# A transformer block on one core: the wide group of the down projection in reverse order, separate buffers for weight sums, a fifth place for split weights, and VectorE in place of GpSimd behind the direct down tiles

## The chip, the core and the metric

The kernel runs on one core of a Trainium2 chip. TensorE (PE in the profile) multiplies, with its weight loads shown as PEld; VectorE (DVE), ScalarE (ACT) and GpSimd (POOL) work elementwise; SyncE (SP) issues nearly all transfers. Each engine runs its own instructions strictly in order, and they wait for each other by semaphores. Tiles lie in SBUF (128 partitions); products accumulate in eight PSUM banks. The metric is the device time of one execution in microseconds. Three runs of the kernel before took 1105.82, 1107.14 and 1108.59 us.

## The reference

One encoder layer on 256 tokens and 16 meta tokens, 2048 channels, all in float32:

```
h = concat(meta, x)
hn = rmsnorm(h);  proj = hn @ w_in
out_a = neighbourhood attention, out_b = latent attention
h = h + concat(rmsnorm(out_a), rmsnorm(out_b)) @ w_out
x2 = rmsnorm(h)
gc = conv_b + sum_i conv_w[i] * shifted(x2 @ w_gate)     # width 3
h = h + (silu(gc) * (x2 @ w_up)) @ w_down                # 5632 inner columns
return h without the meta rows
```

The change touches the last part, above all `@ w_down`: 5632 = 44 x 128 rows of weights, 2048 = 16 x 128 output columns.

## The kernel before

**Split weights.** Each float32 weight is taken apart into a high part of reduced width (`whi`, written by ScalarE, L250) and a low part (`wlo`, the weight minus its high part, written by VectorE, L254). A product of a weight block and an activation is then three products: high x high, high x low, low x high. Weights come in pieces of up to 1024 columns. A piece is loaded into a weight buffer (`raws`; tiles named `raw`, `more_raw`, `halves`), then split by `split_hi` and `split_lo` into one of four places of each kind (`his`, `los`); the weight buffer is free when the low part is done, the place when TensorE has used it. Late in the kernel there are fourteen weight buffers: five `raw`, one `more_raw`, and eight in `halves`, memory that the activations of the gate and up products leave.

**Seven products for eight.** A part of `w_up` and of `w_down` is computed by a scheme with seven block products in place of eight, which needs sums of weight quarters (`weight_sums`, VectorE additions) and sums of activations (`value_sums`, stored in DRAM as `s_up` and `s_down` and loaded again into the tiles `sin` and `sums`, the slots `s_parts`). In `w_up` five groups of four output tiles are done in this way. `w_down` has three parts. The middle group (columns 1024 to 1535) and the wide group (columns 0 to 1023) use the scheme, in 22 row pairs each; the last four output tiles are done directly, m = 0 to 3, 44 blocks each ("direct tiles"). A wide pair has 512-column quarters and seven times three products (`MM`, L290). Its sums are partly made long before, in DRAM, and loaded (tiles `early`): an even pair ("both") loads two sums and computes one buffer of further ones, an odd pair ("third") loads one half and computes two buffers.

**Order.** TensorE's order is a list of pieces: gate and up tiles with the five groups mixed in, then gate and up mixed with the middle group, then the wide group mixed with the pieces of the direct tiles. All other engines' order comes from a planner (`Flow`): every piece of work is a thread that asks for buffers (`Slots`, first come first served), waits for events and then for an engine at an estimated cost; the planner always issues what can start first, by priority among equals. In `load_pair` a pair takes its buffers for weights and for sums together, when its first load is planned. The low-part split (`split_lo`) goes ahead of the sums when it is less than two or three pieces ahead of TensorE. `LANDING` is the planner's time for a load to arrive.

**Direct tiles.** Tiles 0 to 2 take two products a block (`mm2`, L2040 and L2041): the high weights against high and low activations side by side, 512 columns, then the low weights against 256. Tile 3 takes three products of 256 (`mm3`, L713 to L715). `down_out` ends a tile: for tiles 0 to 2 ScalarE copies both halves of the bank into row buffers (`mt`, twelve), GpSimd (L278) adds them, multiplies by the norm's scale and adds the residual; for tile 3 VectorE reads the bank, multiplies and adds. Then the row goes to DRAM.

Of the kernel before, what the change touches and what calls it, by code (L numbers as in the profile page):

```python
# [15 lines left out]
P = 128  # L16
# [201 lines left out]
def encoder_block(ctx: ExitStack, tc: tile.TileContext, io):  # L218
# [103 lines left out]


    combined = Slots(tiles(wpool, 1, [P, PW], "sums"))

# [50 lines left out]
    class RowPair:  # L376
# [55 lines left out]
    s_parts = Slots([])  # L432
    pieces = []
# [71 lines left out]
    def down_pairs(of, src, q):  # L505
        out = []
        for g in range(FC // 2):
            r = RowPair(src[g], g, q, of)
            r.first, r.last, r.near = g == 0, g == LAST, False
            out += [(p, "scheme", r, 0) for p in r.pieces]  # L510
        return out
# [47 lines left out]
    def load_pair(r):  # L559
        def load_S():  # L560
            if r.near:
                r.ev_S = ev_near[r.g]
                return
            if r.of == "mid" and r.g in last_S:
                yield last_S[r.g][1]
                r.S = last_S[r.g][0][0]
                fl.set(r.ev_S)
                return
            r.S = yield from one(s_parts)
            src, saved = saved_sums["up" if r.of == "up" else "down"][r.g]  # L570
            yield saved
            yield "sp", 600
            load(r.S, src, r.ev_S, nc.sync)

        q = r.q
        if r.wide:
# [36 lines left out]
    def weight_sums(r):  # L613
        yield r.loaded
        q = r.q
        if r.wide:
            low, up, t, m = (r.at[k] for k in ("lower", "upper", "two", "more"))
            if r.mode == "both":
                yield r.summed[0]
                yield from TT(m[:, :q], low[:, :q], t[:, :q], ALU.add)  # L620
# [3 lines left out]
            else:  # L624
                yield r.first_loaded
                yield from TT(m[:, :q], up[:, :q], up[:, q:], ALU.add)
# [6 lines left out]
            return  # L633
        t, raw = r.at["sums"], r.at["raw"]
        if r.mode == "third":
# [1236 lines left out]
    near, ev_near = [None] * (KC // 2), [Event() for _ in range(KC // 2)]  # L1872
    act = mts = None

    def mlp_buffers():

        nonlocal act, mts
        yield ev_s2t
# [75 lines left out]
    def value_sums(dst, saved, a, b, place=None):  # L1954
# [53 lines left out]
    def down_out(m, ps):  # L2008
        o = yield from one(mts)
        o_ = o[:, :SEQ]  # L2010
        if m < KC - ST - 1:
            t = yield from one(mts)
            yield from ACT(o_, ps[:, :SEQ], AF.Copy)
            yield from ACT(t[:, :SEQ], ps[:, SEQ:], AF.Copy)
            fl.put(acc, ps)
            yield from PTT(o_, t[:, :SEQ], o_, ALU.add)
            fl.put(mts, t)
            yield from PTT(o_, o_, s_2[:, :SEQ], ALU.mult)
            yield from PTT(o_, o_, hT[ST + m][:, :SEQ], ALU.add)
        else:  # L2020
            yield from TT(o_, ps[:, :SEQ], s_2[:, :SEQ], ALU.mult)
            fl.put(acc, ps)
            yield from TT(o_, o_, hT[ST + m][:, :SEQ], ALU.add)
        if m < KC - ST - 1:
# [22 lines left out]
    def mlp_weights():  # L2047
        pss, f = [], 0
        for p, kind, which, q in work:
# [57 lines left out]
    def scheme_products(p, r):  # L2107
# [31 lines left out]
        if p is r.pieces[-1]:  # L2139
            if not r.near:  # L2140
                if r.S is not near[-1]:
                    fl.put(s_parts, r.S)
# [301 lines left out]
```

## Time and profile before

| | |
|---|---|
| median of three runs | 1107.14 us |
| time of the profiled execution | 1107.99 us |
| its span | 1106.0 us |
| TensorE, VectorE, ScalarE, GpSimd busy | 99%, 92%, 68%, 14% |
| granted TensorE clock | 1.0 |
| moved by DMA | 265.35 MB, mean 240 GB/s |
| share of TensorE in the chain that ended last | 83% |

Busy shares are means over stages with different limits, so the stages have to be read one by one. The attention part lies before some 400 us, gate, up and the five groups up to 770, the middle group up to 942, the wide group with direct tiles from there to 1092, and the end of the last direct tile after it. A matmul's end is modelled and reaches over the start of the next, so that products which follow each other without a gap show a TensorE busy all the time; what a product costs is the distance between two starts.

### The profile page before, as it was taken

To read this page: it belongs to the slowest core of one execution; us is meant where nothing else is said; L and a number is where in the kernel's file an instruction comes from. 1 tells how busy PE (TensorE), PEld (TensorE's weight loads), DVE (VectorE), ACT (ScalarE), POOL (GpSimd) and SP (SyncE) were. 2 spreads that over 40 slices of the span, in tenths; PEclk is the share of its full clock that TensorE was granted. 3 is DMA by queue.
4 is the path that set the end of the run, shared out by engine and by line. 5 is a ranking of instruction groups with operands and counts; after the bars stand their busy time and mean duration, and the time that the engine had idled before them with its cause. 6 is when DMAs were issued, how large, how long until landed. Compare 5 with 4: busy or idle time off the path is not lost.

```text
span 1106.0 us, 22349 instructions
## 1 busy us (share of the span) xinstructions
PE 1095.7 (99%) x8164; PEld 1046.2 (95%) x8164; DVE 1016.9 (92%) x1922; ACT 750.8 (68%) x1514; POOL 149.6 (14%) x217
## 2 busy tenths in 40 slices
PE   9999999999999999999999999999999999999998
PEld 9999999999999999999999999999999999887777
DVE  8979888888878989999999999999999998999997
ACT  8788979798647776656656666665666665766664
POOL 3211222322433400000000000000000000304011
PEclk9999999999999999999999999999999999999999
DMA  8765678667877887665747668667888879699891
GB/s 325 253 230 175 194 226 228 173 195 183 257 204 209 237 283 270 213 205 184 255 161 227 208 208 276 216 220 258 277 307 295 286 260 359 233 337 318 274 313 62
DMA packets 82470, 265.35 MB, mean 240 GB/s; under 512 B 9304, under 2 KB 13016, under 8 KB 82360
## 3 DMA queue, kind: packets, MB, share of 16 engines
q1 hardware_dynamic: 78600, 254.08, 67.6%
q0 software_dynamic: 3472, 9.57, 5.4%
q8 instruction: 64, 1.05, 0.4%
q14 instruction: 46, 0.38, 0.1%
q10 hardware_dynamic: 288, 0.27, 0.1%
HBM read 245.39 MB, written 35.13 MB: 254 GB/s over the span
## 4 chain that ended last, share of the span: by engine, by line
PE 83%; DVE 7%; ACT 4%; DMA 3%; issue 2%; POOL 0%; DVEq 0%; SPq 0%; ACTq 0%; POOLq 0%
PE bank L290 23%; PE bank L713 15%; PE bank L714 15%; PE bank L715 15%; PE bank L2040 10%; PE bank L2041 5%; DVE wlo L254 4%; PE bank L296 2%; ACT whi L250 1%; DMA raw<-early 1%; DVE scr L262 1%; ACT scr L250 1%; DMA raw<-in_w_cq 1%; DMA halves<-early 1%; DVE halves L254 1%
## 5 line engine op out<-in xcount | busy, mean ns | idle before, releaser
L250 ACT ACTIVATE whi<-raw 128x512 fp32r<-128x512 f32 (+2 forms) x513 | 383.0, 767 | 152.4 <-PE bank L714 48.7
L254 DVE TENSOR_TENSOR wlo<-raw,whi 128x512 fp32r<-128x512 f32 (+2 forms) x513 | 445.1, 886 | 29.1 <-ACT whi L250 25.4
L713 PE MATMUL bank<-hl,whi 128*128 128x258 f32 (+1 forms) x1208 | 347.7, 288 | 0.0
L714 PE MATMUL bank<-hl,whi 128*128 128x258 f32 (+1 forms) x1208 | 343.7, 285 | 0.0
L715 PE MATMUL bank<-hl,wlo 128*128 128x258 f32 (+1 forms) x1208 | 343.3, 284 | 0.2
L715 PEld LDWEIGHTS bank<-hl,wlo 128*128 128x128 f32 x1208 | 229.7, 190 | 1.0 <-DVE wlo L254 0.6
L714 PEld LDWEIGHTS bank<-hl,whi 128*128 128x128 f32 x1208 | 229.3, 190 | 0.1
L713 PEld LDWEIGHTS bank<-hl,whi 128*128 128x128 f32 x1208 | 228.3, 189 | 0.4
L290 PE MATMUL bank<-whi,act 128*128 128x256 f32 (+1 forms) x600 | 152.9, 306 | 0.0
L2040 PE MATMUL bank<-hl,whi 128*128 128x512 f32 x384 | 136.5, 395 | 0.0
L290 PEld LDWEIGHTS bank<-whi,act 128*128 128x128 f32 x600 | 105.0, 189 | 6.2
L2041 PE MATMUL bank<-hl,wlo 128*128 128x256 f32 x384 | 107.6, 280 | 0.0
L278 POOL TENSOR_TENSOR mt<-mt,mt 128x256 f32<-128x256 f32 x3 | 13.5, 4496 | 646.6 <-ACT mt L250 646.6
L290 PE MATMUL bank<-wlo,act 128*128 128x256 f32 (+1 forms) x300 | 91.7, 306 | 0.0
L2040 PEld LDWEIGHTS bank<-hl,whi 128*128 128x128 f32 x384 | 72.1, 188 | 14.8
L250 ACT ACTIVATE whi<-halves 128x1024 fp32r<-128x1024 f32 (+1 forms) x68 | 62.4, 933 | 34.1 <-PE bank L290 16.7
L290 PE MATMUL bank<-whi,sin 128*128 128x256 f32 (+1 forms) x264 | 76.3, 333 | 0.0
L254 DVE TENSOR_TENSOR wlo<-halves,whi 128x1024 fp32r<-128x1024 f32 (+1 forms) x68 | 72.9, 1099 | 2.9 <-ACT whi L250 2.8
L2041 PEld LDWEIGHTS bank<-hl,wlo 128*128 128x128 f32 x384 | 72.4, 189 | 0.0
L250 ACT ACTIVATE whi<-more_raw 128x1024 fp32r<-128x1024 f32 (+2 forms) x58 | 49.9, 871 | 25.1 <-PE bank L714 9.3
L290 PEld LDWEIGHTS bank<-wlo,act 128*128 128x128 f32 x300 | 56.7, 189 | 2.8
L254 DVE TENSOR_TENSOR wlo<-more_raw,whi 128x1024 fp32r<-128x1024 f32 (+2 forms) x58 | 57.0, 994 | 2.4 <-ACT whi L250 2.4
(311 smaller groups left out, 2163.1 us busy)
## 6 DMA issues: line engine op xcount, KB each, us to landing
raw<-in_w_gate SPq DMA_DIRECT2D x74, 512.0 KB, 4.8
raw<-in_w_in SPq DMA_DIRECT2D x52, 512.0 KB, 4.9
raw<-in_w_up SPq DMA_DIRECT2D x43, 512.0 KB, 4.9
raw<-in_w_up_s SPq DMA_DIRECT2D x34, 512.0 KB, 4.4
raw<-in_w_out SPq DMA_DIRECT2D x32, 512.0 KB, 5.3
sin<-s_down SPq DMA_DIRECT2D x30, 512.0 KB, 6.5
s_down<-sums SPq DMA_DIRECT2D x22, 512.0 KB, 4.4
raw<-in_w_down_m SPq DMA_DIRECT2D x18, 512.0 KB, 5.5
```

What stands on the lines that cost most here:

```text
L250: nc.scalar.activation(out, in_, f, **kw)
L254: nc.vector.tensor_tensor(out, a, b, op)
L262: nc.vector.scalar_tensor_tensor(out, a, s, b, op0, op1)
L278: nc.gpsimd.tensor_tensor(out, a, b, op)
L290: nc.tensor.matmul(o, l, r, start=start, stop=stop)
L296: nc.tensor.transpose(o, i, ident[:n, :n])
L713: nc.tensor.matmul(ps, whi, xhi, start=start, stop=False)
L714: nc.tensor.matmul(ps, whi, xlo, start=False, stop=False)
L715: nc.tensor.matmul(ps, wlo, xhi, start=False, stop=stop)
L2040: nc.tensor.matmul(ps, whi, x, start=start, stop=False)
L2041: nc.tensor.matmul(ps[:, :n], wlo, x[:, 0, :], start=False, stop=stop)
```

## The change

- The wide group goes through its row pairs from the last (21) to the first (0). The activation sums of the pairs 19, 20 and 21, which the middle group has used last, stay in their three places (`kept_S`); they are no longer loaded for the wide group, and those of 20 and 21 are no longer saved.
- Weight sums get slots of their own, `made`: first `more_raw` alone, then also the last two of the eight in `halves`. `raws` keeps five, later eleven. A pair takes sum buffers when its sums are computed, not when it is loaded.
- Once the middle group's result is read from the banks, a thread takes all twelve row buffers, waits for the low part of the wide group's sixth piece, gives four back and turns the memory of the other eight into a fifth place for high parts and a fifth for low parts.
- Direct tiles 0 to 2 take three products a block and are ended by VectorE as tile 3 is.
- `LANDING` is 3200 instead of 2600.

```diff
-LANDING, SAVING = 2600.0, 2500.0
+LANDING, SAVING = 3200.0, 2500.0
+RING_AT = 5
...
+    made = Slots([])
...
-                fl.put(raws, self.at[kind])
+                by_sums = kind in ("more", "sums") or kind == "two" and self.mode == "third"
+                fl.put(made if by_sums else raws, self.at[kind])
...
-        for g in range(FC // 2):
+        order = range(FC // 2) if of == "mid" else range(LAST, -1, -1)
+        for g in order:
...
+                kept_S[r.g] = r
+                fl.set(ev_kept[r.g])
+                return
+            if r.of == "down" and r.g > LAST - 3:
+                yield ev_kept[r.g]
+                r.ev_S = kept_S[r.g].ev_S
+                r.S = kept_S[r.g].S
                 return
...
-            r.at["two"], r.at["more"] = yield raws, 2
             if r.mode == "both":
+                r.at["two"] = yield from one(raws)
...
-            r.at["raw"], r.at["sums"] = yield raws, 2
+            r.at["raw"] = yield from one(raws)
...
+            if r.mode == "both":
+                yield r.summed[0]
+                r.at["more"] = yield from one(made)
+            else:
+                yield r.first_loaded
+                r.at["two"], r.at["more"] = yield made, 2
...
-            fl.put(raws, t[:, a : a + PW])
+            fl.put(raws if 2 * i + a // PW < 8 - 2 else made, t[:, a : a + PW])
...
-        mts = Slots(tiles(mpool, 12, [P, NT], "mt"))
+        mt_rows[:] = tiles(mpool, 3, [P, 4 * NT], "mt")
+        mts = Slots([t[:, i * NT : (i + 1) * NT] for t in mt_rows for i in range(4)])
...
-            fl.put(raws, t)
+            fl.put(made, t)
...
-        fl.spawn(save_sums(dst, saved, parts, place is None and not last))
+        if not last:
+            fl.spawn(save_sums(dst, saved, parts, place is None))
...
-        if m < KC - ST - 1:
-            t = yield from one(mts)
-            yield from ACT(o_, ps[:, :SEQ], AF.Copy)
-            yield from ACT(t[:, :SEQ], ps[:, SEQ:], AF.Copy)
-            fl.put(acc, ps)
-            yield from PTT(o_, t[:, :SEQ], o_, ALU.add)
-            fl.put(mts, t)
-            yield from PTT(o_, o_, s_2[:, :SEQ], ALU.mult)
-            yield from PTT(o_, o_, hT[ST + m][:, :SEQ], ALU.add)
-        else:
...
+        yield from TT(o_, ps[:, :SEQ], s_2[:, :SEQ], ALU.mult)
+        fl.put(acc, ps)
+        yield from TT(o_, o_, hT[ST + m][:, :SEQ], ALU.add)
...
-                    if which < KC - ST - 1:
-                        yield from mm2(ps, act[:, f], SEQ, f == 0, f == FC - 1)
-                    else:
-                        yield from mm3(
-                            ps[:, :SEQ], act[:, f, 0, :], act[:, f, 1, :], f == 0, f == FC - 1
-                        )
+                    yield from mm3(
+                        ps[:, :SEQ], act[:, f, 0, :], act[:, f, 1, :], f == 0, f == FC - 1
+                    )
...
+    def mts_to_ring():
+        yield mts, 12
+        yield scheme[RING_AT][0].ready[0]
+        for i in range(4):
+            fl.put(mts, mt_rows[0][:, i * NT : (i + 1) * NT])
+        for i, (slots, name) in enumerate(((his, "whi_more"), (los, "wlo_more"))):
+            t = mpool.tile([P, 4 * NT], F32R, tag=f"mt{i + 1}", name=name)
+            fl.put(slots, t[:, :PW])
...
+        fl.spawn(mts_to_ring())
```

TensorE's order stays as it was up to the direct tiles but for the buffers' names. Two places show what moves on other engines.

SP, which issues the loads, at the start of the wide group; `in_w_down_s` are its weights, `in_w_down` those of the direct tiles, `early` stored weight sums, `s_down` activation sums. Before:

```order
L543 DMA raw_83<-in_w_down_s 128x1024
L543 DMA halves_11164<-in_w_down_s 128x512
L543 DMA sin_5456<-s_down_113 128x1024
L543 DMA halves_11164<-early_135 128x1024
L543 DMA halves_11043<-in_w_down_s 128x1024
L543 DMA raw_80<-early_136 128x512
L543 DMA raw_80<-in_w_down_s 128x512
L543 DMA sin_5457<-s_down_114 128x1024
L543 DMA halves_11086<-in_w_down 128x1024
```

and now:

```order
L548 DMA halves_11117<-in_w_down_s 128x1024
L548 DMA raw_83<-early_156 128x512
L548 DMA raw_83<-in_w_down_s 128x512
L548 DMA raw_82<-in_w_down_s 128x1024
L548 DMA halves_11034<-in_w_down_s 128x512
L548 DMA halves_11034<-early_155 128x1024
L548 DMA raw_84<-in_w_down 128x1024
L548 DMA halves_11078<-in_w_down_s 128x1024
L548 DMA halves_11078<-early_154 128x512
```

The two loads of activation sums that stood between the first weights are gone; the first one, for pair 18, now stands eight rows further on, after the weights of the pairs 21 to 18 and part of 17. A "third" pair begins (half of its upper quarters from a stored sum), no longer a "both" one.

VectorE where direct tile 1 ends (its sums are in `bank_72`; `s` is the norm's scale, `res` the residual). Before, only splits and sums stand there:

```order
L254 TENSOR_TENSOR wlo_90<-halves_11043,whi_86 128x1024
L254 TENSOR_TENSOR wlo_91<-halves_11043,whi_87 128x1024
L254 TENSOR_TENSOR wlo_92<-halves_11164,whi_88 128x512
L254 TENSOR_TENSOR wlo_89<-raw_80,whi_85 128x1024
L254 TENSOR_TENSOR wlo_90<-halves_11086,whi_86 128x1024
L254 TENSOR_TENSOR raw_81<-raw_81,raw_82 128x512
L254 TENSOR_TENSOR wlo_91<-more_raw_5458,whi_87 128x1024
L254 TENSOR_TENSOR wlo_92<-halves_11086,whi_88 128x512
```

and now:

```order
L255 TENSOR_TENSOR wlo_more<-raw_83,whi_more 128x1024
L255 TENSOR_TENSOR wlo_92<-halves_11117,whi_88 128x512
L255 TENSOR_TENSOR wlo_89<-halves_11034,whi_85 128x1024
L255 TENSOR_TENSOR mt_5444<-bank_72,s_165 128x256
L255 TENSOR_TENSOR wlo_90<-halves_11155,whi_86 128x1024
L255 TENSOR_TENSOR wlo_91<-raw_82,whi_87 128x1024
L255 TENSOR_TENSOR wlo_more<-halves_11034,whi_more 128x1024
L255 TENSOR_TENSOR mt_5444<-mt_5444,res_4104 128x256
L255 TENSOR_TENSOR wlo_92<-halves_11078,whi_88 128x1024
```

The multiplication from the bank and the addition of the residual stand between low-part splits, and one place in five is the new `wlo_more`.

More of the change, by code (lines that the diff above doesn't have):

```diff
@@ L429, in used @@
             if self.left[kind] == 0:
-                fl.put(raws, self.at[kind])
-    s_parts = Slots([])
+                by_sums = kind in ("more", "sums") or kind == "two" and self.mode == "third"
+                fl.put(made if by_sums else raws, self.at[kind])
+    s_parts, kept_S = Slots([]), {}
+    ev_kept = {g: Event() for g in range(LAST - 2, LAST + 1)}
     pieces = []
@@ L506, in down_pairs @@
         out = []
-        for g in range(FC // 2):
+        order = range(FC // 2) if of == "mid" else range(LAST, -1, -1)
+        for g in order:
             r = RowPair(src[g], g, q, of)
-            r.first, r.last, r.near = g == 0, g == LAST, False
+            r.first, r.last, r.near = g == order[0], g == order[-1], False
             out += [(p, "scheme", r, 0) for p in r.pieces]
@@ L567, in load_S @@
                 fl.set(r.ev_S)
+                kept_S[r.g] = r
[5 more added lines that the diff above has]
+                r.S = kept_S[r.g].S
                 return
             r.S = yield from one(s_parts)
+            if r.of == "mid" and r.g > LAST - 3:
+                assert r.S is not near[-1]
+                kept_S[r.g] = r
+                fl.set(ev_kept[r.g])
             src, saved = saved_sums["up" if r.of == "up" else "down"][r.g]
@@ L624, in weight_sums @@
             else:
-                yield r.first_loaded
                 yield from TT(m[:, :q], up[:, :q], up[:, q:], ALU.add)
@@ L633, in weight_sums @@
             return
-        t, raw = r.at["sums"], r.at["raw"]
+        t = r.at["sums"] = yield from one(made)
+        raw = r.at["raw"]
         if r.mode == "third":
@@ L1872, in encoder_block @@
     near, ev_near = [None] * (KC // 2), [Event() for _ in range(KC // 2)]
-    act = mts = None
+    act = mts = mpool = None
+    mt_rows = []
     def mlp_buffers():
-        nonlocal act, mts
+        nonlocal act, mts, mpool
         yield ev_s2t
@@ L2140, in scheme_products @@
             if not r.near:
-                if r.S is not near[-1]:
+                if kept_S.get(r.g) is r:
+                    pass
+                elif r.S is not near[-1]:
                     fl.put(s_parts, r.S)
```

4 lines of the change are left out of this document (removed).

## The prediction

> **What bounds the kernel now.** I read the page first: who is busy, and where in the span.
>
> ```profile
> PE 1095.7 (99%) x8164; PEld 1046.2 (95%) x8164; DVE 1016.9 (92%) x1922; ACT 750.8 (68%) x1514; POOL 149.6 (14%) x217
> ...
> PEld 9999999999999999999999999999999999887777
> DVE  8979888888878989999999999999999998999997
> DMA  8765678667877887665747668667888879699891
> ```
>
> TensorE is busy everywhere, VectorE nearly so from the middle on, and in the last quarter the transfers fill up too. Since a busy TensorE is not one at its peak, the windows come next; their columns are TensorE, its weight loads, VectorE, ScalarE, GpSimd (busy us and instructions each), the granted clock, the share of the DMA engines, and GB/s.
>
> ```profile
> 500.00:567.00 67.00, 67.00 (x533) 65.59 (x532) 65.92 (x122) 42.11 (x68) 0.00 (x0) 1.00 0.64 213
> 960.00:985.00 25.00, 25.00 (x119) 20.64 (x118) 24.80 (x28) 16.63 (x18) 0.00 (x0) 1.00 0.97 352
> 985.00:1004.00 19.00, 19.00 (x90) 15.51 (x89) 18.97 (x23) 13.84 (x17) 10.16 (x1) 1.00 0.91 307
> 1004.00:1020.00 16.00, 15.29 (x70) 12.22 (x69) 15.93 (x17) 9.65 (x11) 3.15 (x3) 1.00 0.90 300
> 1020.00:1040.00 20.00, 20.00 (x96) 16.53 (x96) 17.89 (x22) 13.01 (x14) 0.00 (x0) 1.00 0.88 307
> 1040.00:1055.00 15.00, 13.86 (x63) 10.81 (x61) 13.16 (x16) 8.98 (x11) 0.00 (x0) 1.00 0.77 262
> 1055.00:1068.00 13.00, 11.39 (x50) 8.96 (x50) 12.97 (x14) 8.42 (x11) 5.33 (x4) 1.00 0.84 294
> ```
>
> Up to 1004 us TensorE has no gap. Between 1004 and 1068, inside the wide group, it has some, while VectorE is full from 960 to 1020. The chain of work that ended last says the same (start, us, what):
>
> ```profile
> 1002.29 2.10 PE bank L290 x9
> 1004.42 1.59 DVE wlo L254
> ...
> 1032.62 7.65 DMA halves<-early
> ...
> 1046.86 7.30 DMA raw<-early
> ...
> 1060.65 5.09 DMA raw<-early
> ...
> 1073.04 8.34 PE bank L290 x36
> ```
>
> It is TensorE's before 1004, VectorE's low-part subtractions and three late loads of stored weight sums until 1068, and TensorE's again to the end. How much this costs is in the view of waits from 925 us on (total us, times, longest):
>
> ```profile
> ACT whi L250 <- PE bank L290: 29.2, 41, 2.3
> ...
> PEld bank L290 <- DVE wlo L254: 6.8, 8, 1.5
> PE bank L290 <- DVE wlo L254: 4.0, 5, 1.1
> DVE wlo L254 <- ACT whi L250: 3.9, 7, 1.6
> DVE more_raw L254 <- DMA halves<-early: 2.3, 1, 2.3
> ...
> DVE halves L254 <- DMA raw<-early: 1.5, 1, 1.5
> ```
>
> TensorE waits 4.0 us for low parts, its weight loads 6.8 us; the loads stop a little earlier than the products do, so the loss lies between, and I take 5 us. That is all that better order in the wide group can give back. VectorE in turn lost 2.3 + 1.5 = 3.8 us to two late loads there.
>
> **The change part by part.**
>
> *Three products instead of two in direct tiles 0 to 2.* 3 tiles x 44 blocks = 132 blocks. The chain and the timeline have two-product blocks, the timeline also three-product ones of the last tile:
>
> ```profile
> 928.02 0.24 PE bank L2040
> ...
> 938.62 0.24 PE bank L2040
> ```
>
> ```profile
> 1000.05 0.39 PE L2040 MATMUL bank<-act,whi 128*128 128x512 f32 x1
> ...
> 1001.78 0.39 PE L2040 MATMUL bank<-act,whi 128*128 128x512 f32 x1
> ```
>
> ```profile
> 1092.09 0.29 PE L713 MATMUL bank<-act,whi 128*128 128x256 f32 x1
> ...
> 1096.05 0.28 PE L713 MATMUL bank<-act,whi 128*128 128x256 f32 x1
> ```
>
> Thirty blocks in 10.60 us are 0.353 us each, five in 1.73 us 0.346; eleven three-product blocks in 3.96 us are 0.360. So TensorE pays 132 x 0.007 = 0.9 us by the longer stretch and 132 x 0.014 = 1.9 by the shorter, and 0 where it waits anyway; I take 1.0, near the longer stretch. The Trainium skill (TensorE: Matmul & The Clock Gate, Back-to-back issue gap) puts the gap of a product of 256 columns at 262 cycles and of 512 at 518, at 2.4 GHz; three short ones would then be 6 cycles, an estimated 0.3 us in all, dearer. By it the sum would be 0.7 us better; the rows above have twice to three times that, and they decide.
>
> *Finishing those tiles.* Nine GpSimd and six ScalarE instructions go, six VectorE ones come. The nearest VectorE row is one that also reads a bank:
>
> ```profile
> L254 DVE TENSOR_TENSOR mt<-bank,mt 128x256 f32<-128x256 f32 x2 | 0.8, 421 | 0.0
> ```
>
> Six x 0.42 = 2.5 us of VectorE, four of them (1.7 us) in the stretch that is short of it. ScalarE's six are spare: it waits 29.2 us for TensorE to give back places. Against that stands what GpSimd's instructions do to VectorE now:
>
> ```profile
> 1027.97 4.62 DVE L254 TENSOR_TENSOR wlo<-halves,whi 128x1024 fp32r<-128x1024 f32 x4
> ...
> 1062.28 0.69 DVE L254 TENSOR_TENSOR more_raw<-halves 128x512 f32<-128x512 f32 x1
> 1063.00 1.12 DVE L254 TENSOR_TENSOR more_raw<-more_raw,halves 128x512 f32<-128x512 f32 x1
> 1064.04 1.76 DVE L254 TENSOR_TENSOR wlo<-raw,whi 128x1024 fp32r<-128x1024 f32 x1
> 1065.73 1.22 DVE L254 TENSOR_TENSOR wlo<-halves,whi 128x512 fp32r<-128x512 f32 x1
> ```
>
> ```profile
> 1003.39 1.11 DVE L254 TENSOR_TENSOR more_raw<-more_raw,halves 128x512 f32<-128x512 f32 x1
> 1004.42 3.94 DVE L254 TENSOR_TENSOR wlo<-halves,whi 128x1024 fp32r<-128x1024 f32 x3
> ```
>
> ```profile
> 993.79 10.16 POOL L278 TENSOR_TENSOR mt<-mt,mt 128x256 f32<-128x256 f32 x1 [34.09 <-ACT mt L250]
> 1061.48 2.08 POOL L278 TENSOR_TENSOR mt<-mt,mt 128x256 f32<-128x256 f32 x1 [53.83 <-ACT mt L250]
> ```
>
> Undisturbed, 512 columns take 0.69 us and a run of 1024-column splits 4.62 / 4 = 1.16 each. Around the GpSimd work of tile 2 three instructions are longer by 0.43, 0.60 and 0.53, around that of tile 1 four by 0.42 and 0.47: 2.4 us together. So this part is worth -2.4 + 1.7 = -0.7 us of VectorE in the short stretch; its ends are +1.7 (the lengthening has another cause) and -2.4 (the new instructions fall into VectorE's own waits). The Trainium skill (SBUF — State Buffer, Who interferes with whom) has a VectorE instruction with two SBUF inputs and a GpSimd instruction that reads SBUF shut each other out for a whole instruction; the 10.16 us of a GpSimd addition that elsewhere takes 2.08 agrees. The new instruction with a bank as input has one SBUF input, so by that page it disturbs nothing.
>
> *A new wait.* The new instructions stand in VectorE's own queue behind TensorE's last product of the tile. Behind them are low-part splits for which TensorE will wait. By the order they come after the low parts of 2,560 columns (two and a half pieces) beyond those that TensorE needs to end tiles 1 and 2. VectorE waits only if it is further ahead than that, and then can spare it: 0, at most one split (1.2 us) each.
>
> *Wide group reversed, last three sums kept.* Three 512 KB loads and two saves of sums leave SP's queue and the 16 engines.
>
> ```profile
> sin<-s_down SPq DMA_DIRECT2D x14, 512.0 KB, 6.8
> ```
>
> Such a load lands 6.8 us after issue. 5 x 0.52 = 2.6 MB at the 300 GB/s of these windows are 8.7 us of transfer time, most of it just where the share is 0.91 to 0.97. No engine waited for one of these loads, so they count as relief for the late ones, not as a term. In exchange all three places for sums are held until the wide group's first pairs are done; the first reload waits for that, and in SP's queue the weights of later pairs stand behind it. Pair 18 needs it after the pairs 20 and 19 and a direct piece: 2 x 21 products x 0.23 us (8.34 / 36 in the chain) and eight blocks of 0.35 are 12.5 us against 6.8: covered by TensorE's own work; were that gone, TensorE would wait for some us once.
>
> *Own buffers for sums.* Before, a wide pair takes four weight buffers at its first load, all from fourteen. Now a pair takes two or three of eleven, and the sums take places from three others only when computed. 14 / 4 = 3.5 pairs ahead become 11 / 2.5 = 4.4: 0.9 pair, some 5 us of lead, more than either late load was late (2.3 and 1.5 us). Hence I let the 3.8 us go, with 0 as the other end. In the four-column groups and in the middle group the sums have one place of their own, the rest five: the order of the splits there moves by a place or two, TensorE's not at all, and with VectorE at 65.92 of 67 us, TensorE without a gap and the DMA engines at 0.64 nothing is late there: 0, up to +1. The planner's longer landing time adds no instruction; it only shifts where splits and sums stand, which is in the same bounds.
>
> *Fifth place for parts.* ScalarE's 29.2 us for places shrink; VectorE waited 3.9 us for ScalarE, 7 times, mostly outside the stretch. Taking all twelve row buffers meanwhile costs nothing: after the middle group only the direct tiles use them. 0, down to -1.
>
> *Sum.* VectorE gains 3.8 + 0.7 = 4.5 us where TensorE loses 5. Not all of it arrives, since DMA stays at 0.8 or more: I take 3.5, with 0 and 5 as ends. 1108.0 us (this execution: 1106.0 span and 2.0 around it) - 3.5 + 1.0 = 1105.5. It stands 0.85 above the median of 1107.14, so the forecast is **1104.6 us**.
>
> **The rivals.**
>
> *The transfers bind.* Then the 3.8 us stay. For it: 0.97 and 352 GB/s in 960:985. Against: 0.77 in 1040:1055, where TensorE loses. VectorE gains 0.7, TensorE pays 1.0: 1107.14 + 0.3 = 1107.4. The Trainium skill (DMA: Bandwidth & Descriptors, Where 436 GB/s comes from) has some 358 GB/s per core as HBM's limit, which the 352 agrees with.
>
> *Slower: three places for sums.* Every second pair takes two of them, the others one; VectorE may write the next pair's sums only after its low-part split of the former, then ScalarE must make the high part, then VectorE the low: one after the other, 22 times. For it: VectorE already waits for ScalarE up to 1.6 us at a time, and is full. Against: other splits stand between in nearly every case. If each pair shows 0.3 us, 22 x 0.3 = 6.6 us: 1104.6 + 6.6 = 1111.2. At 0.11 us a pair the gain is gone, at 0.27 the kernel is measurably slower.
>
> *VectorE held at the direct tiles.* If TensorE is late at tiles 1 and 2, VectorE stands until a piece of eight blocks ends, 8 x 0.35 = 2.8 us each: 1104.6 + 5.6 = 1110.2 at worst, 1107.5 as a middle.
>
> **How the numbers follow.** 0.3% is 3.3 us, about what a measurement of this kernel can tell from no change: faster is below 1103.8, slower above 1110.5. The forecast gets 0.55, with its own range from 1102.2 (all 5 us back, no extra price elsewhere) to 1106.2; a little over half of it is below 1103.8. Transfers 0.15, sums 0.22, direct tiles 0.08. Faster 0.30; same 0.25 + 0.15 + 0.05 + 0.05 = 0.50; slower 0.17 + 0.03 = 0.20. The range goes from 1102.2 to 1110.0, which leaves out most of the sums' case.
>
> **What would show it.** Right: no wait of VectorE for loads of stored sums after 1000 us; GpSimd without a row-buffer instruction, and no 1024-column split of 1.7 us after the middle group; TensorE's waits for low parts under 2 us; the chain TensorE's through the wide group. Three-product blocks at 0.36 us. Wrong, by the rivals: the same loads in the chain at a share over 0.9; more VectorE waits for ScalarE at sums than 3.9 us; waits of VectorE for TensorE's bank at tiles 1 and 2. A gap of TensorE before 925 us would make all of it wrong, since I hold that nothing changes there.

## The result, and the profile after

The changed kernel takes 1103.94 us, median of nine runs (1103.20 to 1104.88); the kernel before took 1108.59 us in nine runs beside them (1105.82 to 1109.28). The ratio is 0.9963, 95% interval 0.9953 to 0.9972: 4.1 us, or 0.37%, faster; the two medians lie 4.65 us apart. The range holds it, and the forecast of 1104.6 us is 0.7 us off, but by the ratio it is "faster", to which the prediction gave less than to "within 0.3%". (Its line for "faster", 1103.8 us, was drawn from the base of 1107.14 us.) The profiled execution took 1104.88 us, its span is 1103.0 us.

The page after, in the same lines as before (busy us; forty slices; and the chain that ended last by engine):

```profile
PE 1096.2 (99%) x8296; PEld 1053.6 (96%) x8296; DVE 1013.9 (92%) x1928; ACT 752.8 (68%) x1508; POOL 128.1 (12%) x208
...
PEld 9999999999999999999999999999999999988887
DVE  8969887878878989999999999999999989999997
...
DMA  8775678567877778665666667768788879599891
...
PE 87%; DVE 4%; ACT 4%; DMA 2%; issue 1%; SPq 0%; POOL 0%; DVEq 0%; ACTq 0%; POOLq 0%
```

TensorE's share of the chain rose from 83% to 87%. The 132 added products are in its count (8296 against 8164). In three of the last four slices the weight loads' digits are 8 where they were 7. The windows of the wide group show the place (columns as in the prediction):

```profile
960.00:985.00 25.00, 25.00 (x139) 21.64 (x139) 24.89 (x29) 16.09 (x19) 1.26 (x2) 1.00 0.96 340
985.00:1004.00 19.00, 19.00 (x97) 16.00 (x96) 18.93 (x24) 12.92 (x15) 0.54 (x1) 1.00 0.93 309
1004.00:1020.00 16.00, 16.00 (x87) 13.73 (x86) 15.89 (x20) 10.04 (x11) 0.00 (x0) 1.00 0.95 348
1020.00:1040.00 20.00, 20.00 (x112) 17.31 (x111) 19.93 (x22) 13.36 (x15) 0.00 (x0) 1.00 0.88 307
1040.00:1055.00 15.00, 15.00 (x78) 12.69 (x77) 14.83 (x19) 9.54 (x11) 0.00 (x0) 1.00 0.82 301
1055.00:1068.00 13.00, 13.00 (x63) 10.82 (x63) 13.00 (x16) 9.15 (x11) 0.54 (x1) 1.00 0.97 343
```

TensorE has no gap any more. VectorE has none to speak of either: in 1020 to 1040 it is busy for 19.93 us where it was for 17.89. The view of waits from 925 us on has no row in which TensorE or a weight load waits for a low part, and none in which VectorE waits for a load. What is left:

```profile
ACT whi L251 <- PE bank L291: 20.3, 22, 2.3
...
DVE wlo L255 <- ACT whi L251: 4.3, 4, 2.0
...
DVE mt L255 <- PE bank L736: 2.7, 1, 2.7
```

The one wait of VectorE for a bank is that at the very end. The chain is TensorE's from here to the last two VectorE instructions (start, us, what):

```profile
1005.28 8.38 PE bank L291 x36
...
1059.15 9.07 PE bank L291 x39
...
1099.18 0.13 PE bank L736
1099.34 0.44 DVE mt L255
1099.80 0.42 DVE mt L255
```

**A measure that is sharper than the time.** TensorE's work is the same in both kernels up to the last quarter, and whole executions of one kernel lie 1 to 6 us apart. So I compare the stretch from the first product of the 32 direct blocks near 928 us to the last product of the kernel. The timeline has its ends and the end of those 32 blocks (start, us, instruction; the third row is the first product behind the blocks); before:

```profile
927.50 0.40 PE L2040 MATMUL bank<-act,whi 128*128 128x512 f32 x1
...
938.82 0.28 PE L290 MATMUL bank<-whi,sums 128*128 128x256 f32 x1
...
1101.69 0.28 PE L715 MATMUL bank<-act,wlo 128*128 128x256 f32 x1
```

and after:

```profile
929.24 0.28 PE L734 MATMUL bank<-act,whi 128*128 128x256 f32 x1
...
940.76 0.28 PE L291 MATMUL bank<-whi,sin 128*128 128x256 f32 x1
...
1099.02 0.28 PE L736 MATMUL bank<-act,wlo 128*128 128x256 f32 x1
```

With 0.12 us for the last product itself, the stretch went from 1101.81 - 927.50 = 174.31 us to 1099.14 - 929.24 = 169.90 us: 4.41 us shorter. The same rows price the third product: 32 blocks take 11.32 us with two products and 11.52 with three, 0.00625 us a block. All profiles below agree on that, 11.31 or 11.32 us against 11.52. The stretch has 124 of the 132 blocks, so 0.78 us. In the changed kernel TensorE has no wait in it; with two products the work alone would be 169.90 - 0.78 = 169.12 us, and the kernel before lost 174.31 - 169.12 = 5.19 us there. Each stretch is that of one profiled execution; how much it varies between executions of one kernel was not measured.

### The profile page after: what moved, and what is told of

Its sections match the earlier page's. It is cut to its first block, busy times and chain, and to the rows that moved or that the text cites. A ratio compares the mean times of both kernels' runs of the same rounds, so it can differ in the third digit from the quotient of the medians.

```text
span 1103.0 us, 22669 instructions
## 1 busy us (share of the span) xinstructions
PE 1096.2 (99%) x8296; PEld 1053.6 (96%) x8296; DVE 1013.9 (92%) x1928; ACT 752.8 (68%) x1508; POOL 128.1 (12%) x208
## 4 chain that ended last, share of the span: by engine, by line
PE 87%; DVE 4%; ACT 4%; DMA 2%; issue 1%; SPq 0%; POOL 0%; DVEq 0%; ACTq 0%; POOLq 0%
PE bank L291 27%; PE bank L734 16%; PE bank L735 16%; PE bank L736 16%; PE bank L2054 8%; PE bank L2055 4%; PE bank L297 2%; DMA scr<-scr 1%; ACT whi L251 1%; DVE wlo L255 1%; DVE scr L263 1%; ACT scr L251 1%; SPq L548 0%; ACT qraw L251 0%; DMA raw<-in_w_cq 0%
## 5 line engine op out<-in xcount | busy, mean ns | idle before, releaser
L251 ACT ACTIVATE whi<-raw 128x512 fp32r<-128x512 f32 (+2 forms) x492 | 352.2, 736 | 161.9 <-PE bank L735 59.7
L255 DVE TENSOR_TENSOR wlo<-raw,whi 128x512 fp32r<-128x512 f32 (+2 forms) x492 | 405.8, 845 | 29.7 <-ACT whi L251 28.7
L291 PE MATMUL bank<-whi,act 128*128 128x256 f32 (+1 forms) x574 | 143.5, 302 | 0.0
L291 PEld LDWEIGHTS bank<-whi,act 128*128 128x128 f32 x574 | 100.2, 189 | 5.1
L251 ACT ACTIVATE whi<-more_raw 128x1024 fp32r<-128x1024 f32 x69 | 71.8, 1040 | 40.9 <-DVE more_raw L255 22.7
L291 PE MATMUL bank<-wlo,act 128*128 128x256 f32 (+1 forms) x287 | 86.8, 302 | 0.0
L255 DVE TENSOR_TENSOR wlo<-more_raw,whi 128x1024 fp32r<-128x1024 f32 x69 | 82.5, 1196 | 3.2 <-ACT whi L251 3.1
L251 ACT ACTIVATE whi<-halves 128x1024 fp32r<-128x1024 f32 (+2 forms) x58 | 54.4, 953 | 26.0 <-PE bank L291 11.3
L291 PE MATMUL bank<-whi,sin 128*128 128x256 f32 (+1 forms) x248 | 69.0, 325 | 0.0
L255 DVE TENSOR_TENSOR wlo<-halves,whi 128x1024 fp32r<-128x1024 f32 (+2 forms) x58 | 63.9, 1121 | 2.3 <-ACT whi L251 2.2
```

Source lines behind the costliest of these rows:

```text
L251: nc.scalar.activation(out, in_, f, **kw)
L255: nc.vector.tensor_tensor(out, a, b, op)
L291: nc.tensor.matmul(o, l, r, start=start, stop=stop)
```

## The experiments

The change has five parts: the planner's landing time, own places for sums, the reversed group with kept sums, the fifth place, and VectorE's finishing with three products. Each run below has its median and its ratio to the kernel before (with the 95% interval), beside which it ran (1108.50, 1108.33 and 1108.30 us in the three sets). "Loss" is its stretch less 169.12 us (two products) or 169.90 (three): what TensorE still waits. The last column is VectorE's busy time in 960 to 1068 us, of 108.

| kernel | median us | ratio | stretch us | loss us | VectorE us |
|---|---|---|---|---|---|
| before | 1108.59 | 1 | 174.31 | 5.19 | 103.72 |
| changed | 1103.94 | 0.9963 (0.9953 to 0.9972) | 169.90 | 0 | 107.48 |
| changed, without own places | 1104.13 | 0.9964 (0.9951 to 0.9976) | 170.10 | 0.20 | 107.44 |
| changed, without reversal and kept sums | 1105.19 | 0.9969 (0.9959 to 0.9979) | 170.38 | 0.48 | 107.55 |
| changed, without VectorE's finishing | 1104.28 | 0.9965 (0.9952 to 0.9977) | 169.74 | 0.62 | 107.48 |
| changed, without fifth place | 1103.56 | 0.9961 (0.9948 to 0.9973) | 170.46 | 0.56 | 107.07 |
| changed, without landing time | 1104.59 | 0.9966 (0.9954 to 0.9978) | 169.89 | 0 | 107.48 |
| before with landing time | 1106.28 | 0.9984 (0.9975 to 0.9993) | 172.30 | 3.18 | 105.89 |
| before with own places | 1108.71 | 1.0002 (0.9993 to 1.0011) | 173.10 | 3.98 | 106.26 |
| before with reversal and kept sums | 1108.22 | 0.9996 (0.9987 to 1.0006) | 172.71 | 3.59 | 105.42 |
| before with VectorE's finishing | 1106.12 | 0.9976 (0.9967 to 0.9984) | 172.32 | 2.42 | 104.73 |
| before with landing time and VectorE's finishing | 1105.70 | 0.9979 (0.9970 to 0.9988) | 171.63 | 1.73 | 106.11 |
| before with the other three parts | 1104.90 | 0.9974 (0.9963 to 0.9985) | 169.81 | 0.69 | 107.48 |
| changed, two products | 1103.03 | 0.9955 (0.9942 to 0.9969) | 169.66 | 0.54 | 107.46 |

### One part undone

**Own places undone.** Sums are taken from the weight buffers again, at the first load of a pair:

```diff
-                by_sums = kind in ("more", "sums") or kind == "two" and self.mode == "third"
-                fl.put(made if by_sums else raws, self.at[kind])
+                fl.put(raws, self.at[kind])
...
+            r.at["two"], r.at["more"] = yield raws, 2
...
```

> The changed kernel with one part undone: the sums take places among the weight buffers again, all at the first load of a pair. Theory (late stored sums): TensorE lost its 5 us because VectorE waited 3.8 us for two late loads of stored sums, and the own places removed that. Then 2.5 to 3.8 us come back, about 1106.5 to 1107.7 us, VectorE waits for stored-sum loads for 2 us or more after 1000 us, and TensorE waits for low parts for 2.5 us or more. Rival (fewer transfers): the three sums that are neither saved nor reloaded already free the queue; then under 0.8 us comes back, up to 1104.7, and there is no such wait. Rival (fifth place): the same, under 0.8 us.

Measured 1104.13 us. VectorE waits for no stored sum, weight loads for low parts 0.7 us. So my theory, that without the own places the late loads and the loss come back, falls at the first run: the loads are in time for VectorE without them. (ScalarE, which splits stored sums too, waits for two of them in the wide group, 0.33 and 1.69 us, while TensorE loses 0.20 us in all.) Both rivals still stand.

**Reversal and kept sums undone.** The order of the pairs, the loads and the saves are as before:

```diff
-        order = range(FC // 2) if of == "mid" else range(LAST, -1, -1)
-        for g in order:
+        for g in range(FC // 2):
...
-        if not last:
-            fl.spawn(save_sums(dst, saved, parts, place is None))
+        fl.spawn(save_sums(dst, saved, parts, place is None and not last))
...
```

> The changed kernel with one part undone: the wide group goes forward again, and all its sums are saved and loaded (five transfers of 512 KB more). Theory (late stored sums, cured by the own places): 0 to 0.8 us comes back, 1103.9 to 1104.7 us, and TensorE waits for low parts under 1 us after 925 us. Rival (fewer transfers): 8.7 us of transfer time where the engines are over 0.9 busy; then 3 to 4 us come back, 1106.9 to 1107.9, with VectorE waiting 2 us or more for loads.

Measured 1105.19 us, between the two expectations and nearer to the theory; TensorE waits for low parts 0.4 us, and the stretch is 0.48 us longer. The rival, for which VectorE should wait for loads for 2 us or more, falls: there is no such wait.

**VectorE's finishing undone.** Two products a block, ScalarE's copies and GpSimd's three instructions a tile are back:

```diff
-        yield from TT(o_, ps[:, :SEQ], s_2[:, :SEQ], ALU.mult)
-        fl.put(acc, ps)
...
+        yield from ACT(o_, ps[:, :SEQ], AF.Copy)
+        yield from ACT(t[:, :SEQ], ps[:, SEQ:], AF.Copy)
+        fl.put(acc, ps)
+        yield from PTT(o_, t[:, :SEQ], o_, ALU.add)
...
```

> The changed kernel with one part undone: ScalarE and GpSimd finish the direct tiles 0 to 2 again, from two products a block. Theory: TensorE gains about 1.0 us from the shorter blocks; VectorE loses 2.4 us to lengthened instructions and saves 2.5 us of its own. If VectorE has room by now, the kernel is 1.0 us faster (1102.9); if it hasn't, TensorE waits some 0.7 to 1.5 us for low parts and the kernel is between 1103.6 and 1104.7. Rival (the interference was the loss): 2.4 us and more come back as waits of TensorE, 1106 us or more.

Measured 1104.28 us, in the theory's second case by the time; TensorE loses 0.62 us, a little under the 0.7 to 1.5 expected. GpSimd disturbs VectorE as it did before (timeline; GpSimd first, then VectorE):

```profile
995.96 1.42 POOL L279 TENSOR_TENSOR mt<-mt 128x256 f32<-128x256 f32 x1 [34.68 <-ACT mt L251]
997.46 1.61 POOL L279 TENSOR_TENSOR mt<-mt,s 128x256 f32<-128x256 f32 x1
```

```profile
996.80 1.66 DVE L255 TENSOR_TENSOR wlo<-raw,whi 128x1024 fp32r<-128x1024 f32 x1
998.39 1.23 DVE L255 TENSOR_TENSOR halves<-raw,halves 128x512 f32<-128x512 f32 x1
```

1.66 instead of 1.22 us, and 1.23 instead of 0.68. Yet TensorE loses 0.62 us only, less than the 0.78 that its shorter blocks save. So the interference is there and is not by itself a loss.

**Fifth place undone.**

```diff
...
-        fl.spawn(mts_to_ring())
```

> The changed kernel with one part undone: high and low parts have four places each to the end. Theory (late stored sums): 0 to 1.0 us comes back, 1103.9 to 1104.9 us; ScalarE waits longer for TensorE, TensorE for low parts under 1 us. Rival (fifth place): the depth of the ring carries the gain, since a late split is bridged by one more piece ahead; then 3 to 4 us come back, 1106.9 to 1107.9, and TensorE waits for low parts 3 us or more.

Measured 1103.56 us; TensorE waits 0.4 us, its weight loads 1.0 us for low parts. The theory's side; the depth of the ring alone does not carry the gain.

None of these four parts is worth more than 0.62 us, then, as long as the other four are there. That leaves the landing time, which stood in all four, or several parts of which each does for the others.

### One part alone

**Landing time.**

```diff
-LANDING, SAVING = 2600.0, 2500.0
+LANDING, SAVING = 3200.0, 2500.0
```

> The kernel before with one number of the change: the planner takes 3200 ns for a load to land, not 2600. No instruction is added; the order of the splits and sums moves from the third quarter on. Four runs with one other part undone each stayed within 1.3 us of the changed kernel, and this number stood in all of them. Theory A (the planner's estimate carries it: with 2600 ns it puts sums ahead of splits at a place where their load is not there yet): 3 to 5 us faster than before, no wait of VectorE for a stored sum over 0.5 us. Theory B (two or more of the other parts each give TensorE the slack): within 1 us of before, the waits for low parts still 3 us or more.

Measured 1106.28 us, some 2 us faster: between A and B. The prediction had put this number at nothing. The rows of the waits from 925 us on:

```profile
PEld bank L290 <- DVE wlo L254: 4.1, 5, 1.0
...
PE bank L290 <- DVE wlo L254: 2.0, 4, 0.6
...
DVE halves L254 <- DMA halves<-early: 0.5, 1, 0.5
```

The late loads of stored sums shrink from 3.8 to 0.5 us, and TensorE's wait halves, from 4.0 to 2.0. The only edit is the planner's number, so the order it makes is the cause; that it puts other VectorE work ahead of just those sums is how I read its rule, and was not followed sum by sum.

**Own places.**

```diff
-            r.at["raw"], r.at["sums"] = yield raws, 2
+            r.at["raw"] = yield from one(raws)
...
+        t = r.at["sums"] = yield from one(made)
...
```

> The kernel before with one part of the change: own places for computed sums. Theory B (each part alone gives slack, so that the loss goes with any one of them): 2.5 to 5 us faster than before, the late loads of stored sums gone from VectorE's waits. Theory A (the landing time carries it) or two parts needed: within 1 us of before, late loads of 2 us or more.

Measured 1108.71 us: no gain in time. Its waits from 925 us on:

```profile
DVE wlo L254 <- ACT whi L250: 4.9, 10, 1.1
PEld bank L290 <- DVE wlo L254: 4.6, 7, 1.4
...
PE bank L290 <- DVE wlo L254: 2.4, 3, 0.9
...
DVE halves L254 <- DMA halves<-in_w_down_m: 1.4, 1, 1.4
```

The late loads of stored sums are gone, as the prediction said, and the stretch is 1.21 us shorter, not 3.8. VectorE's other waits are no full answer: the 1.4 us for a load of the middle group end at 925.00 us, ahead of the stretch, and of the 4.9 us for ScalarE only 1.1 lie in 960 to 1068 us. In that window VectorE idles 2.54 us less than before and TensorE 1.98 us less (windows below). Behind it TensorE waits once more, 0.94 us, where it waited 0.53 before: a few us earlier GpSimd ends tile 2, and VectorE's instructions beside it are longer, 1.76 and 1.22 us instead of 1.22 and 0.68 (GpSimd, VectorE, TensorE):

```profile
1074.66 1.60 POOL L278 TENSOR_TENSOR mt<-mt,res 128x256 f32<-128x256 f32 x1
```

```profile
1073.90 1.76 DVE L254 TENSOR_TENSOR wlo<-more_raw,whi 128x1024 fp32r<-128x1024 f32 x1
1075.59 1.22 DVE L254 TENSOR_TENSOR wlo<-halves,whi 128x512 fp32r<-128x512 f32 x1
```

```profile
1079.45 0.50 PE L290 MATMUL bank<-wlo,sums 128*128 128x512 f32 x1 [0.94 <-DVE wlo L254]
```

What else keeps the gain at 1.21 us is not shown. In the profiled execution the stretch begins 1.64 us later than before, which takes back the 1.21 us (below); whether the median shows no gain for the same reason is not known.

**Reversal and kept sums** alone, the hunks shown above put into the kernel before.

> The kernel before with one part of the change: the wide group reversed and its last three sums kept, five transfers of 512 KB fewer. Theory B: 2.5 to 5 us faster than before. Theory A or two parts needed: within 1 us of before; VectorE still waits for stored sums 2 us or more, and TensorE for low parts 3 us or more.

Measured 1108.22 us; the stretch is 1.60 us shorter. VectorE's waits for loads fall from 3.8 us of stored sums to 0.3, with 1.0 and 0.3 us for weights of the group instead. By the time it is the case of the other theory, by the waits (TensorE's 1.6 us) it lies between the two.

**VectorE's finishing** alone.

> The kernel before with one part of the change: three products a block in direct tiles 0 to 2, and VectorE finishes them. Theory B: VectorE gets back 0.7 us net and TensorE pays 1.0 us, so this part alone is within 1 us of before, and the late loads of stored sums stay. Rival (the interference of GpSimd is the loss): the 1024-column splits of 1.7 us go and with them most of TensorE's waits: 2 to 4 us faster than before.

Measured 1106.12 us, 2.7 us faster by the ratio: the rival, not what my working gave. The late loads mostly stay (2.8 of 3.8 us), yet TensorE's wait falls to 1.2 us:

```profile
PEld bank L290 <- DVE wlo L254: 3.6, 6, 1.3
...
DVE more_raw L254 <- DMA halves<-early: 2.3, 1, 2.3
...
PE bank L290 <- DVE wlo L254: 1.2, 2, 0.8
...
DVE halves L254 <- DMA raw<-early: 0.5, 1, 0.5
```

What GpSimd had cost is in VectorE's groups by form from 945 to 1085 us (count, busy us, mean ns); before:

```profile
L254 DVE TENSOR_TENSOR wlo<-halves,whi 128x1024 fp32r<-128x1024 f32 x40 | 49.3, 1261 | 0.0
L254 DVE TENSOR_TENSOR wlo<-raw,whi 128x1024 fp32r<-128x1024 f32 x27 | 33.6, 1258 | 0.0
...
L254 DVE TENSOR_TENSOR wlo<-halves,whi 128x512 fp32r<-128x512 f32 x15 | 10.8, 719 | 0.0
```

and with VectorE's finishing alone:

```profile
L254 DVE TENSOR_TENSOR wlo<-halves,whi 128x1024 fp32r<-128x1024 f32 x41 | 49.3, 1230 | 0.8 <-ACT whi L250 0.7
L254 DVE TENSOR_TENSOR wlo<-raw,whi 128x1024 fp32r<-128x1024 f32 x27 | 33.0, 1237 | 0.0
...
L254 DVE TENSOR_TENSOR wlo<-halves,whi 128x512 fp32r<-128x512 f32 x16 | 10.9, 682 | 0.0
```

In these three groups alone 40 x 0.031 + 27 x 0.021 + 15 x 0.037 = 2.4 us; the additions in the same view (three into `more_raw` at 970 instead of 681 ns, four of two halves of one buffer at 795 instead of 685) bring 1.3 more: 3.7 us in all, where the prediction counted 2.4.

### Two and three parts

The four parts tried alone are worth 2.01, 1.21, 1.60 and 2.77 us of TensorE's loss, 7.6 together; only 5.19 were to be had.

**Landing time and VectorE's finishing.**

> The kernel before with two parts of the change: the landing time of 3200 ns and VectorE's finishing of the direct tiles from three products a block. Alone they were worth 1.8 and 2.7 us. Theory C (VectorE is short of time in the wide group; what each part gives VectorE, TensorE gets, and the other parts only move VectorE's waits): the two add up, 1108.3 - 4.5 = 1103.8 us, all of the change; TensorE waits for low parts under 1 us. Rival D (both cure the same waits): no better than the better one, 1105.5 to 1106.2.

Measured 1105.70 us, as rival D has it, and C falls: the two do not add up to the whole change. In the trace they do better than either (TensorE's wait 0.3 us, loss 1.73 us against 3.18 and 2.42), but 1.73 us stay.

**Own places, reversal with kept sums, and fifth place.** GpSimd finishes the tiles, and the landing time is as before.

> The kernel before with the three other parts: own places for sums, the wide group reversed with kept sums, fifth place for parts. Theory C: no more than 1 us faster than before (1107.3 or more), since GpSimd's additions still lengthen VectorE's instructions; TensorE waits 2 us or more. Rival E (depth: the three together give enough lead, which none gives alone): 2 to 4 us faster, 1104.3 to 1106.3, with waits under 1.5 us.

Measured 1104.90 us: rival E. The three give TensorE 4.50 of its 5.19 us back, with GpSimd's interference in place. The window of 960 to 1068 us tells it in one line each. Before:

```profile
960.00:1068.00 108.00, 104.53 (x481) 84.68 (x479) 103.72 (x116) 70.52 (x80) 18.63 (x8) 1.00 0.89 309
```

Own places alone, then VectorE's finishing alone, then the three parts together:

```profile
960.00:1068.00 108.00, 106.51 (x490) 86.44 (x490) 106.26 (x121) 70.95 (x81) 20.84 (x7) 1.00 0.91 315
```

```profile
960.00:1068.00 108.00, 106.85 (x559) 90.48 (x559) 104.73 (x123) 70.75 (x77) 1.64 (x3) 1.00 0.91 317
```

```profile
960.00:1068.00 108.00, 107.53 (x498) 88.14 (x497) 107.48 (x121) 71.42 (x83) 12.85 (x7) 1.00 0.93 324
```

VectorE idles 4.28 us before (108 less its busy time, the third of the five, 103.72), 1.74 with own places, 3.27 with its finishing, 0.52 with the three parts, and that last figure again in the changed kernel. The last two columns of the table split in two: where VectorE idles less than 1 us of the 108, eight rows with the run on two products below, TensorE loses 0.69 us or less, whether GpSimd disturbs it or not; where it idles 1.74 us or more, six rows, the loss is 1.73 us or more. Within the six, idle time does not rank them: VectorE's finishing leaves more idle time than own places (3.27 against 1.74) and less loss (2.42 against 3.98); it also makes VectorE's instructions shorter, by the 3.7 us above.

**Landing time undone.**

> The changed kernel with the landing time back at 2600 ns. Theory C: 1.0 to 1.8 us come back, 1105.0 to 1105.8, and TensorE waits 1 us or more for low parts. Rival D or E (any two of the parts suffice): under 0.5 us, 1104.4 or less, waits under 0.5 us.

Measured 1104.59 us, with no wait of TensorE at all: C falls, D and E hold but for 0.2 us of their bound. The stretch is that of the changed kernel, to 0.01 us.

**Two products again, VectorE finishing.** ScalarE copies the second half of the bank, VectorE adds it:

```diff
+            yield from ACT(o_, ps[:, SEQ:], AF.Copy)
+            yield from TT(o_, ps[:, :SEQ], o_, ALU.add)
             fl.put(acc, ps)
-        yield from TT(o_, ps[:, :SEQ], s_2[:, :SEQ], ALU.mult)
+            yield from TT(o_, o_, s_2[:, :SEQ], ALU.mult)
...
```

> The changed kernel with the blocks of direct tiles 0 to 2 back at two products; VectorE still finishes the tiles, with ScalarE's copy of the second half of the bank and one addition more a tile. This prices the three products by themselves, on a TensorE that does not wait. By the rows of the prediction 132 blocks are 0.9 to 1.9 us shorter, so 1102.0 to 1103.0 us. VectorE pays 3 x 0.33 = 1.0 us more; if it has no room for that, TensorE waits as long and the time stays at 1103.5 to 1104. Rival (a third product costs next to nothing): the same time within 0.4 us with no wait.

Measured 1103.03 us, the edge of what the rows gave, but the reason is mixed: the blocks save 0.78 us of the stretch, 0.54 us of it is lost to waits of TensorE for low parts (the view of waits has 0.3 us, weight loads 1.4), and 0.24 us are left. So the rival falls by the blocks, not by the time. The run is faster than the kernel before (0.9955). Against the changed kernel the intervals overlap, and the stretch differs by 0.24 us; the 0.9 us between the medians are not explained by it. In the profiled executions the stretch begins 1.74 us earlier than in the changed kernel.

## Why the prediction was right or wrong

- **The number.** It came out of a gain of 2.5 us (3.5 less 1.0) on a base of 1107.14 us. By the medians of nine runs the gain was 4.65 (4.1 by the ratio, 4.41 by the stretch) and the base 1108.59: the gain was taken 2.15 us too small and the base 1.45 us too low, which nearly cancels. That the forecast came within 0.7 us is luck; by my gain and the better base it would have been 1106.1 us, at the top of its own range.
- **Five us that TensorE can get back.** Right: 5.19 by the stretch, all of it regained. "Not all of it arrives, since DMA stays at 0.8 or more", by which I took 3.5, was the step that failed. The share did stay (0.82 to 0.97 in the windows after) and VectorE waited for no load. The transfers-bind rival fell with it.
- **Three products.** 0.83 us for 132 blocks, against 1.0 taken and 0.9 by the longer stretch. All of it is paid, since TensorE does not wait. The Trainium skill (TensorE: Matmul & The Clock Gate, Back-to-back issue gap) gave an estimated 0.3; the trace has nearly three times that. The rows in the prediction, 7 and 14 ns a block, are three to six times that estimate, not "twice to three times" it.
- **Finishing the tiles.** The mechanism was right, its size was not. Around the two tiles whose rows I read I found 2.4 us; over all three and by means of groups it is 3.7. The new instructions cost VectorE less than their 0.42 us: in one place the next one starts 0.33 us later (995.85 and 996.18 us in the run with this part alone). So VectorE gets an estimated 3.7 - 6 x 0.33 = 1.7 us, not 0.7. TensorE gets 2.77, before it pays 0.78; why more than VectorE's 1.7 is not shown. The sum held that part at +0.3 us of time; alone it shortened the stretch by 1.99 us.
- **Own buffers.** "Hence I let the 3.8 us go": the loads did come in time, but the step from VectorE's waits to TensorE's time failed. Alone the part gave 1.21 us; VectorE idled 2.54 us less in 960 to 1068, TensorE 1.98 us less, it waited 0.94 us behind that window, and what took the rest of the 3.8 us stays open.
- **Landing: no term.** Wrong alone (2.0 us), right beside the other four (0.01 us in the stretch).
- **Reversal and kept sums as mere relief, fifth place 0 to -1.** In the changed kernel they carry 0.48 and 0.56 us. Alone the first gave 1.60 us. The fifth place alone was not tried.
- **What the sum had wrong in kind.** I added the parts as if each owned its piece of the loss. For the most part they replace each other: undone one at a time they bring back 0 to 0.62 us of loss, although together they had taken away 5.19, and once VectorE idles less than 1 us in the window hardly anything is left to be had. That every one acts by giving VectorE time or lead is how I read these figures; no run moved VectorE's idle time and nothing else. Nor is it shown of all: own places, kept sums and fifth place together gave 4.50 us, where the first two, each alone, add up to 2.81.
- **A new wait, the three places for sums, VectorE held.** None came: the only wait of VectorE for a bank is the 2.7 us of the last tile, and it waits 4.3 us for ScalarE, 3.9 before, none of it in 960 to 1068 us.
- **No gap before 925 us.** Right from 430 us on, where TensorE is busy all the time in every profile, to 0.01 us.

In the attention part, before 430 us, the profiles do differ, and the stretch begins between 927.23 and 929.70 us. The changed kernel has two waits for transfers in its chain there (start, us):

```profile
173.75 7.16 DMA scr<-scr
...
233.16 7.01 DMA scr<-scr
```

The stretch begins 1.74 us later in the changed kernel, and so the two spans differ by 3.0 us where the stretches differ by 4.41. Whether those two waits make the late start is not shown: with landing time and VectorE's finishing the chain has two such waits, and the stretch begins at 927.97 us; with own places alone it has none, and the stretch begins at 929.14 us. The order of the work is the same there but for the buffers used. With own places alone the stretch begins 1.64 us later than before, with the reversal alone 1.20 us later; these two are the ones whose medians show no gain, but each start is that of one execution. What sets that start, the memory that buffers lie in or chance, was not tried.

What stays open beside it: which of the own places, the kept sums and the fifth place makes the three work together where the first two do less alone. Every edit also moves the planner's order in the whole wide group, so that a part's price holds in its surroundings alone.

## What to carry to other kernels

Where a nearly full engine feeds another, do not add up the parts of a change: here they replaced each other, and little was left to gain where the feeding engine had less than 1 us of idle time in the stretch. That idle time tells when the gain ends, not which part is worth more. Undo each part and do each alone before you say which one counts; by the times, undoing alone would have said "none", doing alone "two of four". When effects are 0.1% of the time, measure between two products in the trace as well, and on more than one execution if you can.

## What was not expected of the hardware

In the kernel before, GpSimd's addition for tile 1 stood for 10.16 us, from 993.79 us on, while VectorE's instructions with two inputs ran back to back. The timeline of VectorE has them at their usual length during that time (2.35 us for two splits):

```profile
998.13 2.35 DVE L254 TENSOR_TENSOR wlo<-halves,whi 128x1024 fp32r<-128x1024 f32 x2
1000.40 2.35 DVE L254 TENSOR_TENSOR wlo<-raw,whi 128x1024 fp32r<-128x1024 f32 x2
1002.67 0.68 DVE L254 TENSOR_TENSOR more_raw<-halves,halves 128x512 f32<-128x512 f32 x1
```

Only from 1003.39 us on, beside that addition's end and GpSimd's next two instructions, was VectorE slowed: one instruction took 0.42 us more and the next three 0.47 us more together. The Trainium skill (SBUF — State Buffer, Who interferes with whom) calls the ports that the two engines share an exclusive lock, and has a VectorE instruction with two SBUF inputs contend with a GpSimd instruction that reads SBUF. The 10.16 us agree with that for GpSimd. VectorE's instructions were longer only by a part of a GpSimd instruction's length (0.44 and 0.55 us beside 1.42 and 1.61 with VectorE's finishing undone), so no row shows them shut out for the whole of one, as the prediction had it.
